# A decoder trunk on one core: the split parts of the feed-forward weights start at 256 pairs of places instead of one

## The chip, the core and the metric

The kernel runs on one core of one Trainium2 chip. The metric is the device time of one execution in microseconds. TensorE (PE in the profile) multiplies; its weight loads are counted apart as PEld; ScalarE is ACT, VectorE is DVE, GpSimd is POOL, SyncE (SP) issues the transfers.

## The reference

Four layers of a decoder on 256 tokens of 1024 features, all float32. Each layer adds half a SwiGLU feed-forward, a mixer (stick-breaking attention, MoBA, multi-head latent attention, then stick-breaking again) and a second half feed-forward; a norm closes the trunk.

```python
def swiglu(x, w_gate_up, w_down):
    g, u = jnp.split(x @ w_gate_up, 2, axis=-1)
    return (jax.nn.silu(g) * u) @ w_down
...
    for i in range(DEPTH):
        h = h + 0.5 * swiglu(rms_norm(h, norm_ffn1[i]), ffn1_w_gate_up[i], ffn1_w_down[i])
        hn = rms_norm(h, norm_mix[i])
...
        h = h + mix
        h = h + 0.5 * swiglu(rms_norm(h, norm_ffn2[i]), ffn2_w_gate_up[i], ffn2_w_down[i])
    return rms_norm(h, final_norm)
```

D_FF is 2816, so a layer's two feed-forwards hold most of the products.

## The kernel before

**Float32 by two parts.** TensorE multiplies in float32r. Every weight w is split exactly into a high part (ScalarE copies it into a float32r buffer, line 314) and a low part (VectorE subtracts the high part from w, line 321). The activations are split the same way. A product is hi·hi + hi·lo + lo·hi.

**Chunks and pieces.** Weights come in chunks of up to 128 x 2048 values, one transfer each, into one of four `raw` buffers (line 225). `Chunk` (lines 284 to 333) cuts a chunk into two pieces; each takes one of six pairs `whi`/`wlo` of 1024 columns (`parts`, line 226). Every piece starts at column 0 of both its buffers, and row block k stands at k·w from there (`get`, lines 324 to 327).

**The feed-forward's products** (`wide`, lines 432 to 435). For each pair of a 128 x 128 block of weights and a 128-row block of activations there are two matmuls, each with a weight load of its own: the high part against high and low activations side by side (512 columns, line 434), then the low part against the high activations (256 columns, line 435). `x2` holds the normed input so (8 row blocks), `a2` the gated activations (22 row blocks). Gate-up walks 22 chunks of 8 row blocks x 2 column blocks, down 16 chunks of 11 row blocks, in each of 8 feed-forwards: 8 x (352 + 176) = 4224 pairs of matmuls.

```python
def wide(o, wh, wl, m2, first, last):
    nc.tensor.matmul(o, wh, m2.rearrange("p a b -> p (a b)"), start=first, stop=False, skip_group_check=True)
    nc.tensor.matmul(o[:, :SEQ], wl, m2[:, 0, :], start=False, stop=last, skip_group_check=True)
```

**The mixers' products.** `w_proj` with `mm3` (lines 426 to 430) has weights stationary and three matmuls of 256 columns to a block. `x_proj` (lines 462 to 480; its matmuls are lines 475 to 477) has the activations stationary and the split weights moving, 288 to 512 columns wide.

**Places in SBUF.** Tiles are laid out in the order in which they are made, each start rounded up to 32 bytes: `raw`, `parts`, `mids`, `probs`, `nats` (5), `turned`, `squares` (2), `gh`, and then `x2` and `a2`. All before `gh` are whole multiples of 256 bytes long; `gh` takes 8628 bytes, rounded to 8640, which is 192 more than a multiple of 256. So, counted modulo 256 bytes, a weight block stands 64 bytes after the row block of `x2` or `a2` that it is multiplied with, for the high and the low part alike, in all of the feed-forward and in `w_proj`; in `x_proj`, where the roles are exchanged, the stationary operand stands 192 bytes after the moving one.

**Order.** `Program.emit` lists the instructions by estimated costs, at build time: each engine's next is the ready one with the lowest priority number. Buffers taken and given back (`Slots`) are part of it, so a room with fewer buffers can change the order. `square` (line 340) takes one of the `squares` for each row block of a norm's sum of squares; line 345 adds it up, and lines 403 to 408 make the norm from it. `nats` serves the attention's operands and the result.

Of the kernel before, what the change touches and what calls it, by code (L numbers as in the profile page):

```python
# [28 lines left out]
ZC = SEQ + P  # columns of a head's scores that causality leaves  # L29
# [10 lines left out]
HALF = MAXC // 2  # L40

# Gains in one table, 128 rows of a norm to a column.
# [9 lines left out]
class Slots:  # L52
    """Room for a number of like buffers; some of them are kept from work that can wait."""

    def __init__(self, aps):
        self.aps = list(aps)
        self.free = list(range(len(self.aps)))
# [11 lines left out]
class Buf:  # L69
    """A buffer that the first op of its use takes and the last one gives back."""  # L70
# [7 lines left out]
class Op:  # L78
    """A run of instructions: `ways` has its cost and its emitter for each engine that can do it."""
# [6 lines left out]
class Program:  # L86
    """The program as a graph of short runs of instructions. `emit` puts them in order by a list
    scheduling on estimated costs: each engine's next is the ready one with the least priority
    number, which is the tensor engine's nominal time (us) at the op's place."""
# [32 lines left out]
    def copy(self, cols, fn, deps=(), n=1, **kw):  # L122
        """fn(engine's copy) by whichever of ScalarE and VectorE comes to it first."""
        return self.either({"ACT": (n * 0.095 + 0.00083 * cols, lambda: fn(self.on_act)),
                            "DVE": (n * 0.07 + 0.00104 * cols, lambda: fn(self.on_dve))}, deps, **kw)

    def emit(self):
# [3 lines left out]
        events = []  # time, number, op that becomes ready or buffer that becomes free  # L131
# [58 lines left out]
def fast(n, cols=SEQ):  # L190
    """Time of n float32r products."""
    return n * (max(cols, 256) / 2400 + 0.0025)
# [3 lines left out]
def trunk_kernel(ctx: ExitStack, tc: tile.TileContext, a: dict, out: bass.AP, nsub: int = 3 * DEPTH):  # L196
# [23 lines left out]
    # ---- room on the chip  # L220
    def room(n, shape, name, dt=F32):
# [4 lines left out]
    parts = Slots([(cp.tile([P, HALF], F32R, name=f"whi{i}"), cp.tile([P, HALF], F32R, name=f"wlo{i}"))  # L226
                   for i in range(6)])
    mids = room(3, [2 * ZC], "mid")
    probs = room(2, [2, ZC], "prob")
    nats = room(5, [512], "nat")  # L230
    turned = room(4, [4, SEQ], "turned")
    squares = room(2, [SEQ], "sq")
# [3 lines left out]
    # The normed rows and the activations: a row block's high parts, then its low ones.  # L236
    x2 = cp.tile([P, NT, 2, SEQ], F32R, name="x2")
    a2 = cp.tile([P, NF, 2, SEQ], F32R, name="a2")
# [6 lines left out]
    # In a mixer the activations' room holds the heads' outputs, then split softplus or latents.  # L245
# [11 lines left out]
    # ---- the tensor engine's clock rises with work: zeros, until the first data come  # L257
# [6 lines left out]
    # ---- constants  # L264
# [8 lines left out]
    # jp[p, i] = i - p  # L273
# [9 lines left out]
    # ---- the weights: DMA, then an exact split of each float32 value into two float32r parts  # L283
    class Chunk:
        """`n` row blocks of `w` columns, `per` of them to a piece. The program's first chunks come
        and are split in smaller runs of row blocks, between `cuts`, the loads in the order `lead`."""

        def __init__(self, ap, n, w, per, cuts=None, lead=20.0):
            self.w, self.per = w, per
            self.pieces = []  # L290
            self.ready = [None] * n
            raw = Buf(raws)
            load = None if cuts else self.load(ap, raw, 0, n, lead)
            for i in range(0, n, per):
                b = Buf(parts)
                self.pieces.append(b)
                end = min(n, i + per)
                ks = [k for k in cuts or () if i <= k < end] or [i]
                for k, e in zip(ks, ks[1:] + [end]):
                    o = load or self.load(ap, raw, k, e, lead - 3.0 * k)  # L300
                    hi = g.act((e - k) * w, self.hi_fn(raw, b, i, k, e), [o], take=[b] if k == i else [])
                    lo = g.dve((e - k) * w, self.lo_fn(raw, b, i, k, e), [hi], free=[raw])
                    for j in range(k, e):
                        self.ready[j] = lo
# [7 lines left out]
        def hi_fn(self, raw, b, i, k, e):  # L312
            w = self.w
            return lambda: nc.scalar.activation(b.ap[0][:, (k - i) * w:(e - i) * w], raw.ap[:, k * w:e * w], AF.Copy)  # L314

        def lo_fn(self, raw, b, i, k, e):
            w = self.w

            def f():
                s = slice((k - i) * w, (e - i) * w)  # L320
                nc.vector.tensor_sub(b.ap[1][:, s], raw.ap[:, k * w:e * w], b.ap[0][:, s].bitcast(F32))  # L321
            return f

        def get(self, k):
            s = slice(k % self.per * self.w, (k % self.per + 1) * self.w)
            hi, lo = self.pieces[k // self.per].ap
            return hi[:, s], lo[:, s]
# [10 lines left out]
    # ---- norms  # L338
    def square(m, dep, lead):
        """Row block m's share of the mean square; gives the op that adds it."""  # L340
        if m == 0:
            return g.act(SEQ, lambda: nc.scalar.activation(acc, h[:, m, :], AF.Square), [dep], lead=lead)
        b = Buf(squares)
        s = g.act(SEQ, lambda: nc.scalar.activation(b.ap, h[:, m, :], AF.Square), [dep], take=[b], lead=lead)
        return g.dve(SEQ, lambda: nc.vector.tensor_add(acc, acc, b.ap), [s, state["acc"]], free=[b], lead=lead)  # L345

    def prep(m, gain_at, dep, start=False):
        """Row block m of h is final: its gained, split form for the next products, or its share
        of the result, still to be divided by the rms."""
# [12 lines left out]
    def result(m, dep):  # L362
        """Row block m, gained, transposed into the banks of the result."""
# [14 lines left out]
    def rsqrt(v, scale, keep):  # L378
        """(v * scale + EPS) ** -0.5 of a [128, 2] tile, by Newton's method."""
# [3 lines left out]
        # x is -1/2 of the radicand; the first guess comes from its bits.  # L383
# [11 lines left out]
    def norm(scales):  # L395
        """1 / rms of the tokens: as columns (`r`) and along the rows, times the scales (`rb`).
        Gives the ops that make them."""
# [23 lines left out]
    def table(name):  # L421
        """Loads ScalarE's functions, after the last use of those before."""
        state["table"] = g.op("ACT", 1.3, lambda: nc.scalar.preload_act_table_set(name), state["last"], lead=4.0)
        state["last"] = []

    def mm3(o, wh, wl, mh, ml, first, last):
        """o += wh.T @ mh + wh.T @ ml + wl.T @ mh"""
# [4 lines left out]
    def wide(o, wh, wl, m2, first, last):  # L432
        """The same, with the products of the moving operand's low parts in the bank's other half."""
# [6 lines left out]
    def both(o, b, last, take=(), lead=0.0):  # L440
        """o() = the sum of the bank's halves."""
# [3 lines left out]
    def w_proj(chunk, xs, xdeps, keep=0, step=2):  # L445
        """Products with two column blocks of a chunk stationary: a bank [128, 2 x 256], and the
        last op."""
# [14 lines left out]
    def x_proj(chunks, n, cols, xs, xdeps, keep=0):  # L462
        """Products with the activations stationary: two banks [128 tokens, cols], and the last op."""
# [18 lines left out]
    # ---- feed-forward  # L482
    def ffn(l, which, g_next):
# [5 lines left out]
        def gate_up(j, cuts, lead, step):  # L489
            c = Chunk(gu[l, j], NT, 2 * P, NT // 2, cuts, lead)  # L490
# [36 lines left out]
        for m in range(NT):  # L527
            b = bank()
            last = None
            for half in range(2):  # L530
                c = Chunk(dn[l, m, half], FH, P, 6)
# [16 lines left out]
    # ---- shared by the mixers  # L548
    def out_proj(w_o, ot, g_next):
        """The heads' outputs times w_o, onto h."""  # L550
# [9 lines left out]
    def mask_in(o, mask):  # L560
        """The mask of the two diagonal blocks, 256 columns apart."""
# [3 lines left out]
    def head_out(t, p, pdeps, vdeps):  # L565
        """The weighted values of pair t; p: transposed weights [128, 2, 384], keys 0-127 of the 256
        queries, then keys 128-255 of queries 128-255."""
# [18 lines left out]
    # ---- stick-breaking attention  # L586
    def sb_pair(t, s, sdep, vdeps):
        """s: queries and keys of a pair of heads, transposed."""
# [91 lines left out]
    def v_out(half, bs, last, r, n):  # L680
        """Values in their natural layout, times 1 / rms."""
# [3 lines left out]
    # ---- softmax attention of a pair of heads  # L685
    def softmax_pair(t, q, k, deps, vdeps, scale, used):
        """q, k: for each of the two heads, [d, 256] transposed queries and keys."""
# [61 lines left out]
    def rotate(x, cs, n):  # L749
        """Rotary embedding in place: x [128, heads, n], cs: [128, 2, n] (cos twice, sin twice)."""  # L750
# [12 lines left out]
    def turn_heads(x, deps, n, rows, d):  # L763
        """Four blocks of `rows` columns of x[t], transposed, into the tile d."""
# [14 lines left out]
    # ---- MoBA attention: one block holds the sequence, so no past block is ever valid  # L779
# [38 lines left out]
    # ---- multi-head latent attention  # L818
    def mix_mla(j, g_next):
# [3 lines left out]
        # The latents' gained, split, transposed forms.  # L823
# [100 lines left out]
    # ---- the trunk  # L924
# [19 lines left out]
    # ---- the last norm  # L944
# [19 lines left out]
def layouts(x, norm_ffn1, ffn1_w_gate_up, ffn1_w_down, norm_mix, norm_ffn2, ffn2_w_gate_up, ffn2_w_down, sb_w_qkv,  # L964
            sb_w_o, moba_w_qkv, moba_w_o, mla_w_in, mla_q_norm, mla_w_uq, mla_kv_norm, mla_w_ukv, mla_w_o, final_norm):
    """The inputs as the program reads them: every load is of long rows."""
# [14 lines left out]
    for n, gu, dn in (("ffn1", ffn1_w_gate_up, ffn1_w_down), ("ffn2", ffn2_w_gate_up, ffn2_w_down)):  # L981
        # layer, row block, row, gate or up, column block, column
# [8 lines left out]
    def halves(w):  # L991
        """Row blocks in two runs of four, columns in two halves: half, run, row, block, column."""
        return w.reshape(w.shape[0], 2, 4, P, 2, 512).transpose(0, 4, 1, 3, 2, 5).reshape(w.shape[0], 2, 2, P, 2048)

    def outs(w):
        """Pairs of column blocks: pair, row, row block, column of the pair."""
# [44 lines left out]
```

## Time and profile before

| what | value |
|---|---|
| median of 2 runs | 1964.29 us (1962.36 to 1966.22) |
| profiled execution, first to last instruction | 1960.8 us |
| PE busy | 1946.6 us (99%) |
| PEld busy | 1696.5 us (87%) |
| DVE busy | 1452.3 us (74%) |
| ACT busy | 1144.1 us (58%) |

The two runs and the profiled execution are different executions: the runs lie 1.6 to 5.4 us above the profiled span. Matmul records are modelled at their end and reach past the start of the next one, so a matmul's own cost is the distance from its start to the next start.

### The profile page before, as it was taken

The numbers are of one execution on the slowest core, as the hardware profiler recorded it, in microseconds if no ns is written. First come the engines' busy times: TensorE is split into PE (matmuls) and PEld (weight loads), VectorE is DVE, ScalarE is ACT, GpSimd is POOL, SyncE is SP. The second block draws the span as 40 slices with busy tenths as digits, with TensorE's granted clock in tenths as the row PEclk, the third lists the DMA queues.
The fourth block names the chain that finished last, engine by engine and source line by source line (L and its number), as shares of the span: only waits on it lengthen the run. The fifth ranks groups of instructions, "written<-read, shape, count | busy, mean of one in ns | idle before, by whom it ended". The sixth has DMA issues, their size and how long they took to land.

```text
span 1960.8 us, 30578 instructions
## 1 busy us (share of the span) xinstructions
PE 1946.6 (99%) x11681; PEld 1696.5 (87%) x11681; DVE 1452.3 (74%) x2661; ACT 1144.1 (58%) x2119; POOL 0.4 (0%) x5
## 2 busy tenths in 40 slices
PE   9999999999999999999999999999999999999997
PEld 7888989888888878888888888988888888898886
DVE  8777767777777777877677768877677766668864
ACT  7555556555555555655555557755555555665553
POOL 0000000000000000000000000000000000000000
PEclk9999999999999999999999999999999999999999
DMA  8546435546654653554655454355465456435542
GB/s 301 184 146 220 163 129 175 191 147 204 208 181 147 221 181 109 178 188 147 214 199 191 141 178 155 126 197 178 151 213 197 165 168 220 148 125 198 177 151 81
DMA packets 55875, 342.79 MB, mean 175 GB/s; under 512 B 6192, under 2 KB 7088, under 8 KB 26928
## 3 DMA queue, kind: packets, MB, share of 16 engines
q1 hardware_dynamic: 55728, 340.84, 50.6%
q8 instruction: 92, 1.51, 0.3%
q14 instruction: 55, 0.45, 0.1%
HBM read 339.76 MB, written 1.05 MB: 174 GB/s over the span
## 4 chain that ended last, share of the span: by engine, by line
PE 98%; ACT 1%; DVE 0%; DMA 0%; SPq 0%; issue 0%; DVEq 0%; ACTq 0%
PE ps L434 50%; PE ps L435 26%; PE ps L428 3%; PE ps L429 3%; PE ps L430 3%; PE ps L475 3%; PE ps L476 2%; PE ps L477 2%; PE ps L574 1%; PE ps L624 1%; PE ps L733 1%; PE ps L698 1%; PE ps L771 1%; PE ps L596 1%; PE ps L562 0%; PE ps L576 0%
## 5 line engine op out<-in xcount | busy, mean ns | idle before, releaser
L314 ACT ACTIVATE whi<-raw 128x1024 fp32r<-128x1024 f32 (+2 forms) x738 | 703.0, 954 | 729.7 <-PE ps L434 527.3
L321 DVE TENSOR_TENSOR wlo<-raw,whi 128x1024 fp32r<-128x1024 f32 (+2 forms) x738 | 804.2, 1091 | 396.7 <-ACT whi L314 388.6
L434 PE MATMUL ps<-x,whi 128*128 128x512 f32 x2816 | 998.3, 398 | 1.0 <-DVE acc L345 0.8
L435 PE MATMUL ps<-x,wlo 128*128 128x256 f32 x2816 | 791.8, 281 | 0.2 <-DVE wlo L321 0.2
L434 PEld LDWEIGHTS ps<-x,whi 128*128 128x128 f32 x2816 | 529.7, 188 | 132.2 <-ACT whi L314 2.5
L435 PEld LDWEIGHTS ps<-x,wlo 128*128 128x128 f32 x2816 | 528.8, 188 | 1.3 <-DVE wlo L321 1.2
L434 PE MATMUL ps<-a,whi 128*128 128x512 f32 x1408 | 498.8, 398 | 0.0
L435 PE MATMUL ps<-a,wlo 128*128 128x256 f32 x1408 | 395.7, 281 | 0.0
L434 PEld LDWEIGHTS ps<-a,whi 128*128 128x128 f32 x1408 | 264.8, 188 | 65.1
L435 PEld LDWEIGHTS ps<-a,wlo 128*128 128x128 f32 x1408 | 264.4, 188 | 0.0
L443 DVE TENSOR_TENSOR mid<-ps,mid 128x256 f32<-128x256 f32 x416 | 173.5, 417 | 9.6 <-ACT mid L442 9.6
L442 ACT ACTIVATE mid<-ps 128x256 f32<-128x256 f32 x416 | 151.3, 367 | 11.9 <-PE ps L435 11.9
L515 DVE TENSOR_TENSOR mid<-mid 128x256 f32<-128x256 f32 x176 | 74.6, 424 | 14.2 <-DVE mid L443 0.5
L510 DVE TENSOR_TENSOR mid<-mid,rb 128x256 f32<-128x256 f32 x176 | 74.7, 424 | 6.4 <-ACT rb L411 0.9
L475 PE MATMUL ps<-whi,x 128*128 128x512 f32 (+2 forms) x192 | 74.4, 388 | 0.0
L517 DVE TENSOR_TENSOR a<-mid,a 128x256 fp32r<-128x256 f32 x176 | 73.4, 418 | 1.0 <-ACT a L516 1.0
L428 PE MATMUL ps<-a,whi 128*128 128x256 f32 x256 | 73.9, 289 | 0.0
L428 PE MATMUL ps<-x,whi 128*128 128x256 f32 x256 | 73.0, 285 | 0.0
L476 PE MATMUL ps<-wlo,x 128*128 128x512 f32 (+2 forms) x192 | 72.9, 380 | 0.0
L511 ACT ACTIVATE mid<-mid 128x256 f32<-128x256 f32 x176 | 71.8, 408 | 1.8 <-DVE mid L510 1.7
L477 PE MATMUL ps<-whi,x 128*128 128x512 f32 (+2 forms) x192 | 72.7, 379 | 0.0
L429 PE MATMUL ps<-a,whi 128*128 128x256 f32 x256 | 71.5, 279 | 0.0
(128 smaller groups left out, 1636.7 us busy)
## 6 DMA issues: line engine op xcount, KB each, us to landing
raw<-in_ffn_gu SPq DMA_DIRECT2D x173, 1024.0 KB, 4.8
raw<-in_ffn_dn SPq DMA_DIRECT2D x128, 704.0 KB, 4.1
raw<-in_sb_qk SPq DMA_DIRECT2D x16, 1024.0 KB, 4.9
raw<-in_moba_qkv SPq DMA_DIRECT2D x12, 1024.0 KB, 4.8
raw<-in_sb_v SPq DMA_DIRECT2D x8, 1024.0 KB, 4.7
raw<-in_sb_o SPq DMA_DIRECT2D x8, 1024.0 KB, 4.7
raw<-in_moba_o SPq DMA_DIRECT2D x4, 1024.0 KB, 4.8
raw<-in_mla_o SPq DMA_DIRECT2D x4, 1024.0 KB, 5.0
```

What stands on the lines that cost most here:

```text
L314: return lambda: nc.scalar.activation(b.ap[0][:, (k - i) * w:(e - i) * w], raw.ap[:, k * w:e * w], AF.Copy)
L321: nc.vector.tensor_sub(b.ap[1][:, s], raw.ap[:, k * w:e * w], b.ap[0][:, s].bitcast(F32))
L428: nc.tensor.matmul(o, wh, mh, start=first, stop=False, skip_group_check=True)
L429: nc.tensor.matmul(o, wh, ml, start=False, stop=False, skip_group_check=True)
L434: nc.tensor.matmul(o, wh, m2.rearrange("p a b -> p (a b)"), start=first, stop=False, skip_group_check=True)
L435: nc.tensor.matmul(o[:, :SEQ], wl, m2[:, 0, :], start=False, stop=last, skip_group_check=True)
L442: x = g.act(SEQ, lambda: nc.scalar.activation(o(), b.ap[:, SEQ:], AF.Copy), [last], take=take, lead=lead)
L443: return g.dve(SEQ, lambda: nc.vector.tensor_add(o(), b.ap[:, :SEQ], o()), [x], free=[b], lead=lead)
L475: nc.tensor.matmul(o, xs[0][:, k, ts], hi, start=(k == 0), stop=False)
L476: nc.tensor.matmul(o, xs[0][:, k, ts], lo, start=False, stop=False)
L477: nc.tensor.matmul(o, xs[1][:, k, ts], hi, start=False, stop=(k == n - 1))
L510: o = g.dve(SEQ, lambda: nc.vector.tensor_mul(x(), x(), rb[:, 0, :]), [o, rbs[0]])
```

## The change

Each `whi` and `wlo` buffer becomes 64 columns (256 bytes) longer, and a piece starts at a place in it: one of 16 starts, 4 columns (16 bytes) apart, for the high part and one for the low part. `place(i)` gives the i-th of the 256 pairs. Gate-up's pieces go through them in order, the high part's place changing from piece to piece (2 x 176 = 352 pieces, so 96 pairs come twice); down's 256 pieces go through them with the two parts exchanged. All mixers' pieces have the pair (48, 0): the high part 192 bytes in, the low part at the start. `x2` and `a2` move up, right behind `parts`; as the longer buffers are still multiples of 256 bytes, a place is now the distance, modulo 256 bytes, from the row block of activations to the block of weights. To make room, `nats` goes from 5 buffers to 4 and `squares` from 2 to 1.

```diff
+PAD = 64
...
-    parts = Slots([(cp.tile([P, HALF], F32R, name=f"whi{i}"), cp.tile([P, HALF], F32R, name=f"wlo{i}"))
+    parts = Slots([(cp.tile([P, HALF + PAD], F32R, name=f"whi{i}"), cp.tile([P, HALF + PAD], F32R, name=f"wlo{i}"))
                    for i in range(6)])
+
+    x2 = cp.tile([P, NT, 2, SEQ], F32R, name="x2")
+    a2 = cp.tile([P, NF, 2, SEQ], F32R, name="a2")
...
-    nats = room(5, [512], "nat")
+    nats = room(4, [512], "nat")
...
-    squares = room(2, [SEQ], "sq")
+    squares = room(1, [SEQ], "sq")
...
-    x2 = cp.tile([P, NT, 2, SEQ], F32R, name="x2")
-    a2 = cp.tile([P, NF, 2, SEQ], F32R, name="a2")
...
+            self.places = places or [(48, 0)] * (n // per + 1)
...
-            return lambda: nc.scalar.activation(b.ap[0][:, (k - i) * w:(e - i) * w], raw.ap[:, k * w:e * w], AF.Copy)
+            w, o = self.w, self.places[i // self.per][0]
+            return lambda: nc.scalar.activation(b.ap[0][:, o + (k - i) * w:o + (e - i) * w], raw.ap[:, k * w:e * w], AF.Copy)
...
-                nc.vector.tensor_sub(b.ap[1][:, s], raw.ap[:, k * w:e * w], b.ap[0][:, s].bitcast(F32))
+                oh, ol = self.places[i // self.per]
+                n = (k - i) * w, (e - i) * w
+                nc.vector.tensor_sub(b.ap[1][:, ol + n[0]:ol + n[1]], raw.ap[:, k * w:e * w],
+                                     b.ap[0][:, oh + n[0]:oh + n[1]].bitcast(F32))
...
             hi, lo = self.pieces[k // self.per].ap
-            return hi[:, s], lo[:, s]
+            at = k % self.per * self.w
+            oh, ol = self.places[k // self.per]
+            return hi[:, oh + at:oh + at + self.w], lo[:, ol + at:ol + at + self.w]
...
+    def place(i):
+
+        return 4 * (i % 16), 4 * (i // 16)
...
-            c = Chunk(gu[l, j], NT, 2 * P, NT // 2, cuts, lead)
+            at = 2 * ((2 * l + which) * NF + j)
+            c = Chunk(gu[l, j], NT, 2 * P, NT // 2, cuts, lead, [place(at % 256), place((at + 1) % 256)])
...
-                c = Chunk(dn[l, m, half], FH, P, 6)
+                at = 2 * (((2 * l + which) * NT + m) * 2 + half)
+                c = Chunk(dn[l, m, half], FH, P, 6, None, 20.0, [place(at)[::-1], place(at + 1)[::-1]])
```

The number of instructions is the same on every engine, and so are the shapes. On PE the order changes only within the first feed-forward's first five chunks. Before, the first norm's sum (the two matmuls of `onesf` and `acc`) stood after the fourth chunk:

```order
L434 MATMUL ps_68<-x_107,whi_84 128x512
L435 MATMUL ps_68<-x_107,wlo_85 128x256
L434 MATMUL ps_69<-x_107,whi_84 128x512
L435 MATMUL ps_69<-x_107,wlo_85 128x256
L403 MATMUL ps_70<-onesf,acc 128x1 x2
L434 MATMUL ps_71<-x_107,whi_86 128x512
L435 MATMUL ps_71<-x_107,wlo_87 128x256
```

Now it stands twelve matmuls later, among those of the chunk that follows (lines 439, 440 and 408 are the former 434, 435 and 403):

```order
L439 MATMUL ps_71<-x_90,whi_86 128x512
L440 MATMUL ps_71<-x_90,wlo_87 128x256
L408 MATMUL ps_72<-onesf,acc 128x1 x2
L439 MATMUL ps_70<-x_90,whi_86 128x512
L440 MATMUL ps_70<-x_90,wlo_87 128x256
L439 MATMUL ps_71<-x_90,whi_86 128x512
L440 MATMUL ps_71<-x_90,wlo_87 128x256
```

No other matmul changes its place among the weights' products. On ACT, at the same time of the program, squares and splits before:

```order
L354 ACTIVATE x_107<-gh 128x256 x2
L344 ACTIVATE sq_105<-gh 128x256
L314 ACTIVATE whi_78<-raw_74 128x512
L344 ACTIVATE sq_104<-gh 128x256
L314 ACTIVATE whi_80<-raw_75 128x512
L354 ACTIVATE x_107<-gh 128x256 x2
```

With a single square buffer two splits follow each other (lines 359, 349 and 316 are the former 354, 344 and 314):

```order
L359 ACTIVATE x_90<-gh 128x256 x2
L349 ACTIVATE sq_105<-gh 128x256
L316 ACTIVATE whi_78<-raw_74 128x512
L316 ACTIVATE whi_80<-raw_75 128x512
L349 ACTIVATE sq_105<-gh 128x256
L359 ACTIVATE x_90<-gh 128x256 x2
```

The square that stood between the two splits comes after them.

## Rows read from the trace of the kernel before

**Rows 1.** The page, part 1: busy time by engine, share of the span.
```profile
span 1960.8 us, 30578 instructions
PE 1946.6 (99%) x11681; PEld 1696.5 (87%) x11681; DVE 1452.3 (74%) x2661; ACT 1144.1 (58%) x2119; POOL 0.4 (0%) x5
```

**Rows 2.** The page, part 4: the chain that ended last, by engine and line.
```profile
PE 98%; ACT 1%; DVE 0%; DMA 0%; SPq 0%; issue 0%; DVEq 0%; ACTq 0%
PE ps L434 50%; PE ps L435 26%; PE ps L428 3%; PE ps L429 3%; PE ps L430 3%; PE ps L475 3%; PE ps L476 2%; PE ps L477 2%; PE ps L574 1%; PE ps L624 1%; PE ps L733 1%; PE ps L698 1%; PE ps L771 1%; PE ps L596 1%; PE ps L562 0%; PE ps L576 0%
```

**Rows 3.** Waits of PE: total us, times, longest us.
```profile
PE ps L434 <- DVE acc L345: 0.8, 1, 0.8
...
PE ps L435 <- DVE wlo L321: 0.2, 1, 0.2
```

**Rows 4.** Line 434 in 440 to 490 us: ns min/median/max, first and last start.
```profile
L434 PE MATMUL ps<-a,whi x143: 397/397/398, 439.7 to 489.9; 128*128 128x512 f32 x143
```

**Rows 5.** Timeline of a feed-forward from 501 us: start us, us, instruction.
```profile
501.06 0.28 PE L435 MATMUL ps<-x,wlo 128*128 128x256 f32 x1
501.06 0.19 PEld L434 LDWEIGHTS ps<-x,whi 128*128 128x128 f32 x1
501.17 0.40 PE L434 MATMUL ps<-x,whi 128*128 128x512 f32 x1
501.18 0.19 PEld L435 LDWEIGHTS ps<-x,wlo 128*128 128x128 f32 x1
501.41 0.28 PE L435 MATMUL ps<-x,wlo 128*128 128x256 f32 x1
```

**Rows 6.** Groups by line and form: xcount | busy us, mean ns | idle before.
```profile
L434 PE MATMUL ps<-x,whi 128*128 128x512 f32 x2816 | 998.3, 398 | 1.0 <-DVE acc L345 0.8
L435 PE MATMUL ps<-x,wlo 128*128 128x256 f32 x2816 | 791.8, 281 | 0.2 <-DVE wlo L321 0.2
L321 DVE TENSOR_TENSOR wlo<-raw,whi 128x1024 fp32r<-128x1024 f32 x456 | 557.5, 1224 | 229.9 <-ACT whi L314 228.0
L434 PE MATMUL ps<-a,whi 128*128 128x512 f32 x1408 | 498.8, 398 | 0.0
L435 PE MATMUL ps<-a,wlo 128*128 128x256 f32 x1408 | 395.7, 281 | 0.0
L443 DVE TENSOR_TENSOR mid<-ps,mid 128x256 f32<-128x256 f32 x416 | 173.5, 417 | 9.6 <-ACT mid L442 9.6
L517 DVE TENSOR_TENSOR a<-mid,a 128x256 fp32r<-128x256 f32 x176 | 73.4, 418 | 1.0 <-ACT a L516 1.0
```

**Rows 7.** PE groups in 271 to 275.2 us (`w_proj`).
```profile
L428 PE MATMUL ps<-x,whi 128*128 128x256 f32 x13 | 3.6, 276 | 0.0
```

**Rows 8.** PE groups in 297.5 to 307 us (`w_proj`).
```profile
L428 PE MATMUL ps<-a,whi 128*128 128x256 f32 x28 | 7.9, 281 | 0.0
```

**Rows 9.** PE groups in 1701.3 to 1708.1 us (`x_proj`).
```profile
L476 PE MATMUL ps<-wlo,x 128*128 128x512 f32 x11 | 4.3, 394 | 0.0
L475 PE MATMUL ps<-whi,x 128*128 128x512 f32 x11 | 4.3, 392 | 0.0
L477 PE MATMUL ps<-whi,x 128*128 128x512 f32 x10 | 3.9, 388 | 0.0
```

**Rows 10.** Busy time in 30 to 130 us (gate-up).
```profile
core 0: us, PE busy (x) PEld busy (x) DVE busy (x) ACT busy (x) POOL busy (x), PEclk, DMA share, GB/s
30.00:130.00 100.00, 100.00 (x568) 86.83 (x567) 77.57 (x129) 57.91 (x109) 0.00 (x0) 1.00 0.54 188
```

**Rows 11.** Groups by line and form in the mixers, whole span.
```profile
L429 PE MATMUL ps<-a,whi 128*128 128x256 f32 x256 | 71.5, 279 | 0.0
...
L476 PE MATMUL ps<-wlo,x 128*128 128x512 f32 x160 | 62.8, 392 | 0.0
```

More of the change, by code (lines that the diff above doesn't have):

```diff
@@ L284, in trunk_kernel, with __init__ @@
     class Chunk:
-        def __init__(self, ap, n, w, per, cuts=None, lead=20.0):
+        def __init__(self, ap, n, w, per, cuts=None, lead=20.0, places=None):
             self.w, self.per = w, per
+            self.places = places or [(48, 0)] * (n // per + 1)
             self.pieces = []
@@ L312, in hi_fn @@
         def hi_fn(self, raw, b, i, k, e):
-            w = self.w
-            return lambda: nc.scalar.activation(b.ap[0][:, (k - i) * w:(e - i) * w], raw.ap[:, k * w:e * w], AF.Copy)
+            w, o = self.w, self.places[i // self.per][0]
+            return lambda: nc.scalar.activation(b.ap[0][:, o + (k - i) * w:o + (e - i) * w], raw.ap[:, k * w:e * w], AF.Copy)
         def lo_fn(self, raw, b, i, k, e):
@@ L319, in f @@
             def f():
-                s = slice((k - i) * w, (e - i) * w)
-                nc.vector.tensor_sub(b.ap[1][:, s], raw.ap[:, k * w:e * w], b.ap[0][:, s].bitcast(F32))
+                oh, ol = self.places[i // self.per]
+                n = (k - i) * w, (e - i) * w
+                nc.vector.tensor_sub(b.ap[1][:, ol + n[0]:ol + n[1]], raw.ap[:, k * w:e * w],
+                                     b.ap[0][:, oh + n[0]:oh + n[1]].bitcast(F32))
             return f
         def get(self, k):
-            s = slice(k % self.per * self.w, (k % self.per + 1) * self.w)
             hi, lo = self.pieces[k // self.per].ap
-            return hi[:, s], lo[:, s]
+            at = k % self.per * self.w
+            oh, ol = self.places[k // self.per]
+            return hi[:, oh + at:oh + at + self.w], lo[:, ol + at:ol + at + self.w]
         def used(self, ks):
```

## The prediction

> **What bounds the kernel now.** I read the busy shares first, then the chain, then PE's waits. PE is busy for 1946.6 of 1960.8 us [rows 1], and the chain that ended last is PE for 98%, of which lines 434 and 435, the feed-forward's products, are 76% [rows 2]. PE hardly waits for anyone: its longest waits on splits or norms are 0.8 and 0.2 us, once each, at the start [rows 3]. So an edit counts only if it changes how fast matmuls follow each other, or slows VectorE or ScalarE until PE starts to wait.
>
> How fast they follow is the second reading. In a feed-forward 143 matmuls of line 434 start between 439.7 and 489.9 us: 50.2/142 = 353.5 ns for a pair (512 and 256 columns) [rows 4]. The timeline shows how it divides: 0.24 us from the 512-wide start to the next start, 0.11 to 0.12 from the 256-wide one, and each weight load runs while the matmul before it runs [rows 5]. The record of a 512-wide matmul is 398 ns long and of a 256-wide one 281 [rows 6], some 163 ns beyond the next start in both cases. I take that tail as fixed, so a record that is 5 ns shorter means a pitch that is 5 ns shorter.
>
> Now the same shapes elsewhere. The 256-wide matmul of `w_proj` has records of 276 ns in one stretch [rows 7] and of 281 in another [rows 8]. The 512-wide one of `x_proj` has 388, 392 and 394 [rows 9], mean 391.3. The granted clock is 1.00 (the upper level, 2.4 GHz) in the gate-up stretch that I looked at [rows 10]. So the feed-forward's matmuls stand at the slow end of what these shapes do in this trace, by up to 10 ns for 512 columns and 5 for 256. The place of operands is one thing that could make the difference: the feed-forward has its weights 64 bytes after the moving rows (modulo 256), `x_proj` has 192. It is not the only one: `w_proj` has both 276 and 281 at one and the same distance of 64.
>
> **The change part by part.**
>
> *Feed-forward pieces at 256 pairs of places.* 4224 pairs of matmuls, 8448 weight loads (2816 + 1408 of each line, [rows 6]). Nothing in the trace has these pairs of places. Lower end: both matmuls as short as the shortest rows, 388 and 276, so (398 - 388) + (281 - 276) = 15 ns a pair, 4224 x 15 = 63 us gained. Middle: the means of the other shapes, 391.3 and 278.5, give 6.7 + 2.5 = 9.2 ns, 39 us gained. No effect of places: 0. On the other side no steady row is above 398 and 281, so the trace gives no price for a bad place; I bound it by a load that is no longer hidden at one of the 16 distances, 8448/16 = 528 loads, each for the pitch of the shortest matmul that carries a whole load, 276 - 163 = 113 ns, so 60 us lost. Between -63 and +60 I take half of the middle, 4224 x 4.6 = 19 us gained. Reason: an average over all places should lie inside what the shapes do and not at the slow end, where the one pair in use lies now; but `w_proj` shows that part of that difference is not the place.
>
> A rule of the Trainium skill speaks against any gain. The page "TensorE: Matmul & The Clock Gate", Part 2, "Step-by-step: what each phase is for", says that PE has two independent SBUF read ports, one for the moving operand and one for the weight load, so that loading the next weights takes nothing from the running matmul. By that rule no place costs or gives anything and this term is 0; the trace agrees that loads run beside matmuls [rows 5], and leaves open why one shape has records from 388 to 398 ns.
>
> *Mixer pieces at (48, 0).* `w_proj` then has distances 192 and 0 instead of 64, `x_proj` 64 and 0 instead of 192. 1536 matmuls of `w_proj` average about 279 [rows 11]: all at 276 would give 1536 x 3 = 4.6 us, all at 281 would cost 3.1. Of `x_proj` 480 are 512 wide, at 392 [rows 11]: at 388 they give 1.9 us, at 398 they cost 2.9. Together -7 to +6; I take 0.
>
> *The splits at shifted starts.* ScalarE and VectorE do the same instructions. A split of 1024 columns takes VectorE 1224 ns [rows 6]. In 100 us of gate-up VectorE is busy for 77.57 [rows 10]; a chunk lasts 16 pairs x 353.5 ns = 5.66 us and has two splits, so 35 splits share 22.4 idle us: each may grow by 0.64 us, to 1.86, before VectorE binds. A shift of 64 bytes between operands shows nothing: line 517 works on `a2` and `mids`, which are off by that much, in 418 ns, line 443 on aligned tiles and PSUM in 417 [rows 6]. I take 0, hidden under PE.
>
> *One square buffer, four `nats`.* Squares then alternate with VectorE's sums. In the trunk the norm's row is needed only after the next products have begun, and PE's order does not change there. At the start two splits follow each other at once, where a square stood between: PE's waits of 0.8 and 0.2 us [rows 3] are what this can give, and a square more in front of the norm is what it can cost. I take -0.5, bounds -1 to +2.
>
> **The sum.** -19 + 0 + 0 - 0.5 = about -20 us, on a profiled span of 1960.8: 1941. The median of the runs lies 3.5 us above that span, so 1964.3 - 20 = 1944 us.
>
> **The rivals.**
>
> *No effect of places.* For it: `w_proj` has two pitches at one distance, and the rule above says so. Against it: one shape has records from 388 to 398 ns in one program, at two different distances. Time: 1964.
>
> *The places free the feed-forward wholly.* If most pairs of places are as good as the other shapes' rows, the gain is 39 to 63 us: 1901 to 1925, more than 2% (39.3 us, about what a measurement of this kernel can tell from no change). For it: the feed-forward sits at the slow end for its whole length, 398 and 281 as means over thousands of records [rows 6], like a fixed pattern that any shift would break. Against it: 256-wide matmuls fall into the 281 pattern at times whatever came before.
>
> *A bad distance.* The other side: at some distances the weight load and the moving rows meet in the same part of SBUF, and the load is not hidden any more. Place: the feed-forward's loads. Price: 113 ns a load. It decides from 39.3/0.113 = 348 loads on, 4% of 8448, so a single bad distance of the 16 is enough: 1964 + 60 = 2024 us. For it: only two of the 16 distances are in the trace, and distance 0, where both start in the same place, is not. Against it: neither of these two, nor any steady row, shows a load that stands in the open.
>
> VectorE as the new bound would need splits half as long again; I count it with the bad distance.
>
> **How the numbers follow.** Forecast (a gain by about half of the middle, 1925 to 1964) 0.40; no effect 0.26; wholly free 0.21; bad distance 0.13. The first two lie within 2%: 0.66. Faster is 0.21, slower 0.13. The range goes from 1902 (the lower end of the sum) to 1988, beyond no effect and the small costs; it leaves out most of the bad distance. The likeliest case alone: 1925 to 1964. Predicted 1944.
>
> **What would show it.** Right: PE still 99% busy with the same chain; records of lines 439 and 440 (the former 434 and 435) no longer all 398 and 281 but varying from piece to piece, in stretches of 8 to 16 pairs, with a mean between 388 and 398 and between 276 and 281; gate-up stages shorter by some 1%. No effect: the same two numbers in all pieces. Bad distance: a share of 1 in 16 with much longer records and weight loads. Wrong altogether: VectorE above 95% in gate-up and PE waiting for `wlo`, or records above 398 in most pieces.

## The result and the profile after

The changed kernel runs in 1951.78 us (median of 2 runs, 1951.72 to 1951.84) against 1964.29 before: ratio 0.9937, 95% interval 0.9919 to 0.9956. That is 0.6% faster: clear of no change by its interval, and within the 2% called the same. Predicted were 1944 us, with a range of 1902 to 1988. Executions of one kernel differ by up to 4 us, and in six of the thirteen traces of this document, not in the two compared here, the granted clock is 0.50 (the lower level, 1.2 GHz) instead of 1.00 for 3.4 us that begin 11 to 13 us after the start.

The profiled execution spans 1950.1 us, 10.7 less than before. The page's busy times and its chain, the counterpart of [rows 1, 2]:

```profile
span 1950.1 us, 30511 instructions
PE 1935.1 (99%) x11681; PEld 1694.9 (87%) x11681; DVE 1450.4 (74%) x2661; ACT 1146.0 (59%) x2119; POOL 0.4 (0%) x5
...
PE 98%; ACT 1%; DVE 0%; DMA 0%; SPq 0%; issue 0%; DVEq 0%; ACTq 0%
```

PE bounds the kernel as before, and nearly the whole difference lies in how fast matmuls follow each other. The groups by line and form (busy us, mean ns of one, idle before) are the counterpart of [rows 6, 11]; 439 and 440 are the former 434 and 435, 433 to 435 the former 428 to 430, 480 to 482 the former 475 to 477:

```profile
L439 PE MATMUL ps<-x,whi 128*128 128x512 f32 x2816 | 987.2, 395 | 1.7 <-DVE acc L350 1.4 <-ACT whi L316 0.3
L440 PE MATMUL ps<-x,wlo 128*128 128x256 f32 x2816 | 788.4, 280 | 0.2 <-DVE wlo L324 0.2
L324 DVE TENSOR_TENSOR wlo<-raw,whi 128x1024 fp32r<-128x1024 f32 x456 | 557.3, 1223 | 223.8 <-ACT whi L316 222.1
L439 PE MATMUL ps<-a,whi 128*128 128x512 f32 x1408 | 493.3, 394 | 0.0
L440 PE MATMUL ps<-a,wlo 128*128 128x256 f32 x1408 | 394.1, 280 | 0.0
L435 PE MATMUL ps<-a,wlo 128*128 128x256 f32 x256 | 72.4, 283 | 0.0
L434 PE MATMUL ps<-a,whi 128*128 128x256 f32 x256 | 71.8, 281 | 0.0
L481 PE MATMUL ps<-wlo,x 128*128 128x512 f32 x160 | 63.6, 397 | 0.0
```

In the feed-forward the records fell from 398 to 395 and 394, and from 281 to 280. In the mixers they rose: line 434 (the former 429) from 279 to 281, line 481 from 392 to 397. The split of 1024 columns takes as long as before (1223 ns against 1224).

The same stretch of a feed-forward as in [rows 4] (ns min/median/max, first and last start) and the gate-up stretch of [rows 10]:

```profile
L439 PE MATMUL ps<-a,whi x144: 388/394/403, 439.7 to 489.7; 128*128 128x512 f32 x144
```
```profile
30.00:130.00 100.00, 100.00 (x575) 87.57 (x574) 79.95 (x134) 60.49 (x113) 0.00 (x0) 1.00 0.54 192
```

Where every record was 397 or 398, they now go from 388 to 403, and a pair takes 50.0/143 = 349.7 ns instead of 353.5. The clock is 1.00 in both, and VectorE at 80% is far from binding.

Taken apart by the first and last matmul of each stage, the 16 feed-forward stages (8 gate-up, 8 down) are 15.9 us shorter (gate-up from 1004.4 to 993.9, down from 500.3 to 494.9), the four mixers between them 4.9 us longer (from 441.9 to 446.8), and the end 0.3 us longer: -15.9 + 4.9 + 0.3 = -10.7.

A piece lasts 8 pairs in gate-up, so the two windows below each lie inside one piece: first the pair of places (16, 4) at its second visit, then (16, 16), the distance of before (groups of PE in the window, busy us, mean ns).

```profile
L439 PE MATMUL ps<-x,whi 128*128 128x512 f32 x6 | 2.1, 389 | 0.0
L440 PE MATMUL ps<-x,wlo 128*128 128x256 f32 x5 | 1.4, 276 | 0.0
```
```profile
L439 PE MATMUL ps<-x,whi 128*128 128x512 f32 x6 | 2.2, 396 | 0.0
L440 PE MATMUL ps<-x,wlo 128*128 128x256 f32 x6 | 1.7, 281 | 0.0
```

The first is within 1 ns of the shortest rows of before, 388 and 276; the second is close to the old 398 and 281. From start to start the means of the pairs of places go from 340.5 ns a pair of matmuls to 355.2; the mean over all 256 is 349.4.

### The profile page after: what moved, and what is told of

Read it like the earlier page. It is cut to its first block, busy times and chain, and to the rows that moved or that the text cites. A ratio compares the mean times of both kernels' runs of the same rounds, so it can differ in the third digit from the quotient of the medians.

```text
span 1950.1 us, 30511 instructions
## 1 busy us (share of the span) xinstructions
PE 1935.1 (99%) x11681; PEld 1694.9 (87%) x11681; DVE 1450.4 (74%) x2661; ACT 1146.0 (59%) x2119; POOL 0.4 (0%) x5
## 4 chain that ended last, share of the span: by engine, by line
PE 98%; ACT 1%; DVE 0%; DMA 0%; SPq 0%; issue 0%; DVEq 0%; ACTq 0%
PE ps L439 50%; PE ps L440 25%; PE ps L433 3%; PE ps L435 3%; PE ps L434 3%; PE ps L480 3%; PE ps L481 2%; PE ps L482 2%; PE ps L585 1%; PE ps L635 1%; PE ps L744 1%; PE ps L709 1%; PE ps L782 1%; PE ps L607 1%; PE ps L573 0%; PE ps L587 0%
## 5 line engine op out<-in xcount | busy, mean ns | idle before, releaser
L439 PE MATMUL ps<-x,whi 128*128 128x512 f32 x2816 | 987.2, 395 | 1.7 <-DVE acc L350 1.4
L439 PE MATMUL ps<-a,whi 128*128 128x512 f32 x1408 | 493.3, 394 | 0.0
L440 PE MATMUL ps<-a,wlo 128*128 128x256 f32 x1408 | 394.1, 280 | 0.0
L433 PE MATMUL ps<-a,whi 128*128 128x256 f32 x256 | 73.7, 288 | 0.0
L435 PE MATMUL ps<-a,wlo 128*128 128x256 f32 x256 | 72.4, 283 | 0.0
```

The lines of the kernel that those rows point to most:

```text
L433: nc.tensor.matmul(o, wh, mh, start=first, stop=False, skip_group_check=True)
L435: nc.tensor.matmul(o, wl, mh, start=False, stop=last, skip_group_check=True)
```

## Experiments

Three theories stood at first. D: the distance from the moving rows to the weights, modulo 256 bytes, sets the pitch. P: it is the change of place from piece to piece that breaks a slow pattern. L: the gain came from the layout, the order or the rooms. All edits below are to the changed kernel, unless said otherwise.

**One fixed pair for the whole feed-forward, four times.** The edit, here for the first; the others have (16, 16), (16, 4) and (24, 44) in its place, and the second and third also have (16, 16) as the mixers' pair:

```diff
-        return 4 * (i % 16), 4 * (i // 16)
+        return 48, 0
...
-                c = Chunk(dn[l, m, half], FH, P, 6, None, 20.0, [place(at)[::-1], place(at + 1)[::-1]])
+                c = Chunk(dn[l, m, half], FH, P, 6, None, 20.0, [place(at), place(at + 1)])
```

> All feed-forward pieces at the one pair (48, 0), as the mixers' pieces already are: high part 192 bytes after the activations modulo 256, low part 0. Theory D (the distance of each part from the moving rows sets the pitch): in the changed kernel the pieces at this pair ran at 340.6 ns a pair of matmuls against 353.4 before, so 4224 x 12.8 = 54 us less than before, and 5 us more in the mixers: about 1915 us, records near 389 and 276. Theory P (it is the change of place from piece to piece that breaks a slow pattern): one fixed pair falls back to 353.4, about 1969 us. Theory L (the gain came from the new layout, order or rooms, not from the places): as the changed kernel, 1952 us.

> All pieces, the mixers' too, at (16, 16): the layout, the order and the rooms of the changed kernel, but every distance is again 64 bytes as in the kernel before. Theory D: the pitch of before, 353.4 ns a pair, records 398 and 281, and the mixers as before: 1964 us within 3. Theory P: the same. Theory L: 1952 us or less, since the layout is kept.

> All feed-forward pieces at (16, 4), high part 64 bytes and low part 16 bytes on, the mixers' pieces at (16, 16) as before. Theory D: the pieces at this pair ran at 340.5 ns a pair in the changed kernel, so 4224 x 12.9 = 54 us less than before and the mixers as before: about 1910 us. Theory P: 1964 us. Theory L: 1952 us.

> All feed-forward pieces at (24, 44), the pair with the longest pitch in the changed kernel (355.2 ns), the mixers at (48, 0). Theory D: 4224 x 1.8 = 8 us more than before and 5 us more in the mixers: about 1977 us. Theory P: about 1969 us. Theory L: 1952 us.

| feed-forward, mixers | us | ratio to before, interval |
|---|---|---|
| (48, 0), (48, 0) | 1939.2 | 0.9875, 0.986 to 0.989 |
| (16, 16), (16, 16) | 1964.8 | 1.0001, 0.9991 to 1.001 |
| (16, 4), (16, 16) | 1909.6 | 0.9724, 0.971 to 0.9739 |
| (24, 44), (48, 0) | 1943.4 | 0.9896, 0.9881 to 0.991 |

The 512-wide matmuls of the same 50 us of a down stage, for (16, 16), then for (16, 4), whose stage ends at 485 us:

```profile
L439 PE MATMUL ps<-a,whi x143: 397/397/398, 439.7 to 489.8; 128*128 128x512 f32 x143
```
```profile
L439 PE MATMUL ps<-a,whi x134: 389/389/389, 439.8 to 485.0; 128*128 128x512 f32 x134
```

(16, 16) has the layout, the order and the rooms of the changed kernel and the distances of the old one, and its records are those of [rows 4], to the nanosecond. L falls. (16, 4) differs from it by 48 bytes in the place of the feed-forward's low parts and by nothing else, and gains 55 us: a pair of matmuls takes 45.2/133 = 339.8 ns (340.0 over a whole down stage, against 353.3 at (16, 16)), record after record the same 389. A fixed place does that, so P falls as well. It is faster than the kernel before and the changed one.

D holds for these two to 1 us, and misses the other two: (48, 0) should have come to 1915 and came to 1939, (24, 44) to 1977 and came to 1943. So the sweep's number for a single pair of places need not be what that pair does when it stays.

**The rooms and the order alone.** The kernel before with `nats` at 4 and `squares` at 1:

```diff
-    nats = room(5, [512], "nat")
+    nats = room(4, [512], "nat")
...
-    squares = room(2, [SEQ], "sq")
+    squares = room(1, [SEQ], "sq")
```

> The kernel before with only the rooms changed: 4 nats instead of 5, 1 square instead of 2; no places, x2 and a2 at the end of the layout as before (1024 + 2048 bytes earlier, so still 64 bytes off). It has the order of the changed kernel. Theory D (distances alone): as before, 1964 us, within 2. Theory L (order or rooms have a share in the gain): below 1962 us, by as much as that share.

1964.1 us, ratio 1.0002 (0.9993 to 1.0011): no share in the gain that this can show.

**The mixers' places alone.** The sweep stays, the mixers' pieces go back to the old distance:

```diff
-            self.places = places or [(48, 0)] * (n // per + 1)
+            self.places = places or [(16, 16)] * (n // per + 1)
```

> The changed kernel with its sweep in the feed-forward, but the mixers' pieces at (16, 16), the distance of before. Theory D: the mixers' stages took 4.9 us longer in the changed kernel than before (1.5 + 1.8 + 0.3 + 1.3); these come back, so 1952 - 5 = 1947 us. If the mixers' loss came from what the sweep leaves behind (state, order), nothing comes back: 1952 us.

1948.1 us, ratio 0.9921 (0.9908 to 0.9935), 3.6 us less than the changed kernel's 1951.8. Line 434 in its groups:

```profile
L434 PE MATMUL ps<-a,whi 128*128 128x256 f32 x256 | 71.7, 280 | 0.0
L434 PE MATMUL ps<-x,whi 128*128 128x256 f32 x256 | 71.3, 278 | 0.0
```

They are back at 278 to 280, and the four stretches between the stages take 442.5 us, against 446.8 in the changed kernel and 441.9 before: 4.3 of the 4.9 us come back. The mixers' loss is that of their pair (48, 0).

**Distance or address.** Both kernels put 64 bytes ahead of `x2`. The first moves all places by 64 bytes too, so that distances stay as with (16, 4) and addresses do not; the second leaves the feed-forward's weights at (16, 4), so that their addresses stay and the distances do not.

```diff
+    cp.tile([P, 16], F32, name="shift")
     x2 = cp.tile([P, NT, 2, SEQ], F32R, name="x2")
```

> As the run with (16, 4) and mixers (16, 16), but x2 and a2 start 64 bytes later, and so do all places: (32, 20) and (32, 32). All distances between weights and activations are those of that run, all addresses are other ones modulo 256. Distance theory: the same time, 1910 us, 340 ns a pair. Address theory (each operand's own address modulo 256 counts): some other pitch between 340 and 355 ns, 1910 to 1973 us, most likely near the mean of the sweep, 349, so 1947 us.

> As the run with (16, 4), the weights at the same addresses, but x2 and a2 start 64 bytes later (mixers at (32, 32), which keeps their distance at 64). The distances in the feed-forward become 0 and 208 bytes instead of 64 and 16, while high and low part keep theirs from each other. Distance theory: the pitch of the pair (0, 52), 348.9 ns in the sweep, so 1964 - 4224 x 4.5 = 1945 us, within the 350 and 340 that a fixed pair may lock to. If only the weights' addresses or the distance of the high from the low part count: 340 ns, 1910 us.

1909.0 us (ratio 0.9725, 0.971 to 0.974) and 1945.5 us (0.9909, 0.9895 to 0.9922). The matmuls of the first and the second in the same window (line 440 is 439 here):

```profile
L440 PE MATMUL ps<-a,whi x133: 389/389/389, 439.8 to 484.7; 128*128 128x512 f32 x133
```
```profile
L440 PE MATMUL ps<-a,whi x145: 392/393/396, 439.6 to 489.9; 128*128 128x512 f32 x145
```

Same distances, other addresses: the same 389. Same weight addresses, same distance between high and low part, other distance to the moving rows: 392 to 396. So it is the distance between the weights and the rows that stream past them that counts, in this test by a shift of 64 bytes. The second run is also where the sweep was right about a pair that stays: 348.9 ns both times.

**The same pair in all shapes.** Mixers at (16, 4) as well:

> All pieces, the mixers' too, at (16, 4). The feed-forward as with mixers at (16, 16): 340 ns a pair, 1909.6 us in all. If the pair is good for every shape, w_proj goes from a mean pitch of 116 to 113.3 ns and x_proj from 229 to 227: 1536 x 2.6 + 696 x 2 = 5 us less, about 1904 us. If a distance is good for one order of matmuls only, the mixers move by up to 5 us either way: 1905 to 1915 us.

1912.6 us (0.9735, 0.9719 to 0.9751), about 3 us more than with the mixers at (16, 16), though the two intervals overlap. The traces are clearer: the stretches between the stages take 444.8 us instead of 442.3, and in `w_proj` the records are longer than the 278 that the mixers at (16, 16) have just shown:

```profile
L434 PE MATMUL ps<-x,whi 128*128 128x256 f32 x256 | 72.0, 281 | 0.0
```

A pair that is good for 512 and 256 columns in turn is not good for three times 256.

**Why (48, 0) and (24, 44) miss.** In the trace of (48, 0) the feed-forward has two pitches, each for nearly whole stages. The first line is from the third gate-up stage, the second from the sixth (the last count of such a line is that of a sample):

```profile
L439 PE MATMUL ps<-x,whi x273: 395/395/396, 514.7 to 609.9; 128*128 128x512 f32 x137
...
L439 PE MATMUL ps<-x,whi x280: 389/389/390, 1284.9 to 1379.7; 128*128 128x512 f32 x140
```

Start to start this is 350.0 ns in the first five feed-forwards and 340.0 in the last three, but for stretches of up to 32 pairs of matmuls at the start of some gate-up stages, at one and the same pair of places. Two more runs went after that. In the first only the mixers' pair is another one, (16, 16); in the second the first two chunks of each feed-forward stand at (16, 4) as well:

```diff
-            c = Chunk(gu[l, j], NT, 2 * P, NT // 2, cuts, lead, [place(at % 256), place((at + 1) % 256)])
+            c = Chunk(gu[l, j], NT, 2 * P, NT // 2, cuts, lead, [(16, 4)] * 2 if j < 2 else [place(at % 256), place((at + 1) % 256)])
```

> Feed-forward at (48, 0), mixers at (16, 16). With the mixers at (48, 0) the feed-forward ran at 350.0 ns a pair until the third mixer and at 340.0 after it, for whole stages. If the distance alone set the pitch, one value would hold throughout; if the pitch is a pattern that is caught when a stage begins and then kept, the stages divide otherwise between 340 and 350 now that other work stands before them, and the time lies between 1964 - 54 = 1910 us (all at 340) and 1964 - 14 = 1950 us (all at 350).

> As the run with (48, 0) in the feed-forward and (16, 16) in the mixers, but the first two chunks of every feed-forward stand at (16, 4), the pair that ran at 340 ns everywhere. If the pitch of (48, 0) is a pattern that is caught and then kept, all stages start from the fast one and stay in it: 340 ns from the first feed-forward on, about 1910 us instead of 1934. If the change from 350 to 340 ns at the third mixer has another cause (what runs, or what data stand, from there on), the first five stages still run at 350: about 1934 us.

The first gave 1933.9 us (0.9847, 0.9832 to 0.9862), with the same division as in the run at (48, 0) everywhere: the places of the mixers' weights did not change it, against what the pattern theory expected. The second gave 1933.1 us (0.9839, 0.9823 to 0.9855), neither the 1910 of a pattern that always stays fast nor the old division. After two slow feed-forwards, fast and slow ones now alternate. Its third gate-up stage, slow in both runs before, and its sixth, fast in both:

```profile
L439 PE MATMUL ps<-x,whi x295: 389/389/389, 509.7 to 609.7; 128*128 128x512 f32 x148
...
L439 PE MATMUL ps<-x,whi x292: 395/395/395, 1274.6 to 1376.5; 128*128 128x512 f32 x146
```

So the third mixer alone is not the cause. The same pieces with the same data take either pitch, though nothing was changed but the places of the first two chunks of each feed-forward. The timeline of its second gate-up stage (start us, us) shows a pattern being left, inside these first chunks at (16, 4), where the norm's small matmuls stand between:

```profile
317.07 0.39 PE L439 MATMUL ps<-x,whi 128*128 128x512 f32 x1
317.30 0.28 PE L440 MATMUL ps<-x,wlo 128*128 128x256 f32 x1
317.42 0.39 PE L439 MATMUL ps<-x,whi 128*128 128x512 f32 x1
317.65 0.28 PE L440 MATMUL ps<-x,wlo 128*128 128x256 f32 x1
317.76 0.50 PE L408 MATMUL ps<-onesf,acc 128*128 128x1 f32 x4
318.12 0.48 PE L439 MATMUL ps<-x,whi 128*128 128x512 f32 x1
...
318.56 0.39 PE L439 MATMUL ps<-x,whi 128*128 128x512 f32 x1
318.78 0.28 PE L440 MATMUL ps<-x,wlo 128*128 128x256 f32 x1
318.90 0.39 PE L439 MATMUL ps<-x,whi 128*128 128x512 f32 x1
```

Ahead of it the steps are 0.35 us a pair (346.7 ns over the nine pairs before 317.42), behind it 0.34 (340.1 over the ten from 318.56 on). So (16, 4) did not run at 340 ns everywhere, as the last expectation has it. In its own run, too, it begins each gate-up stage behind a mixer at 347 ns. The pair (24, 44) begins these stages at 360.0 ns and goes over to 346.7 behind the norm's last small matmuls. Here are (16, 4), (48, 0) and (24, 44) at the start of the second gate-up stage of their first runs, then (24, 44) and (48, 0) further on in it:

```profile
L439 PE MATMUL ps<-x,whi x16: 392/392/392, 305.7 to 310.9; 128*128 128x512 f32 x16
L439 PE MATMUL ps<-x,whi x17: 389/389/389, 311.3 to 316.7; 128*128 128x512 f32 x17
L439 PE MATMUL ps<-x,whi x16: 402/402/403, 310.9 to 316.3; 128*128 128x512 f32 x16
...
L439 PE MATMUL ps<-x,whi x316: 393/393/393, 322.7 to 431.9; 128*128 128x512 f32 x158
L439 PE MATMUL ps<-x,whi x316: 395/395/396, 322.6 to 432.9; 128*128 128x512 f32 x158
```

This explains (24, 44) as well: the sweep met it twice, for five and for eight pairs of matmuls, once near either pitch (347.5 and 358.4 ns), and the mean of these few made it the longest; when it stays, the short pitch holds for all but the starts of the first gate-up stage and of those behind mixers.

The traces also show where the pitch changes. Each gate-up stage has two breaks, the norm's sums (line 408) and its two transposes (line 413). Behind a mixer they stand after the 20th and the 32nd pair of matmuls, behind another feed-forward after the 20th and the 28th, in the first feed-forward after the 38th and the 52nd. With (48, 0) throughout, the pitch changes within a few pairs of one of these breaks and nowhere else in the seven gate-up stages after the first, and the pitch behind the transposes goes on through the down stage.

In the last run (16, 4) holds for the first 32 pairs. Where a feed-forward follows another one, the transposes leave four pairs of it; these run at 340 ns, and (48, 0) takes 340 over and keeps it, all three times. Where it follows a mixer, (48, 0) begins right behind the transposes, at 350 ns, all four times, and in the first feed-forward the transposes stand well inside (48, 0), with 350 on both sides. So the fast pattern was kept wherever it ran when the places changed, and the miss of 23 us comes from the other five. That is read from the traces; no run moves the norm's matmuls. Why the transposes leave 350 ns behind them in five feed-forwards of the runs at (48, 0) and 340 in the last three stays open.

## Why the prediction was right, and where it was not

*What bounds the kernel.* Right: PE at 99%, the same chain, and no new wait but one of 0.3 us at the start.

*The sum.* Forecast were about 20 us; the medians give 12.5 and the traces 10.7. Between the traces, 3.6 of the missing 8.8 us are the feed-forward with its start (-19.5 forecast, -15.9 measured), 4.9 the mixers and 0.3 the end.

*The feed-forward's places.* Forecast 4.6 ns a pair and 19 us; measured 15.9/4224 = 3.8 ns and 15.9 us. The reason given, that an average over all places lies inside what the shapes do and the pair in use lies at the slow end, is what the pieces show: 349.4 on average, between 340.5 and 355.2, with the old distance at 353.3 when it stays. The tail taken as fixed bears out: from (16, 16) to (16, 4) the two records lose 8 and 5 ns and the pitch 13.3. The half taken off was argued from `w_proj`'s two pitches at one distance; the runs at (48, 0) show two pitches at one distance in the feed-forward too. That it should be a half, no row said: that 19 lies so near 15.9 is luck in part.

*No effect of places.* Refuted by (16, 16) against (16, 4): 48 bytes, 55 us. The rule of the Trainium skill weighed there (page "TensorE: Matmul & The Clock Gate", Part 2, "Step-by-step: what each phase is for") says that loading the next weights takes nothing from the running matmul. What the prediction drew from it, that no place costs or gives anything, does not hold for these products; the measurement decides. Whether the rule itself fails is not shown: that reads of weights and of moving rows get in each other's way is my reading of the distance that matters, and no run separates the load from the rest.

*The mixers.* This is the term that was mis-sized: 0 was taken between bounds of -7 and +6, and it was +4.9, of which 4.3 us came back when their pair was undone. I had taken gains and losses to cancel with no row for it; `w_proj` and the 512-wide matmuls of `x_proj` both lost.

*Splits, rooms, order.* The splits are right at 0: 1223 ns for 1024 columns. The gain of 0.5 us from the order did not come: PE's waits on splits and the norm, 0.8 and 0.2 us before, are 1.4, 0.3 and 0.2 after, and with the rooms alone the kernel took 1964.1 us.

*The places free the feed-forward wholly.* Not with the sweep, but with one pair that stays: (16, 4) gains 55 us, inside the 39 to 63 worked out for it. The rows of other products gave that floor rightly, 389 and 276 against 388 and 276. The argument against it, that the 281 pattern comes at times whatever came before, had no row; in the feed-forward what stands before does bear on the pitch, as the runs at (48, 0) show.

*A bad distance.* Did not come: in the sweep no pair of places has a mean above 355.2 ns, and the longest pitch that was kept, 360.0 ns at (24, 44) behind a mixer, is 6.7 ns above (16, 16); a load in the open had been priced at 113.

## To carry to other kernels

Where PE is full and the same shape has different record lengths in different stretches, the place of the stationary operand against the moving one is worth a few runs, even 16 bytes of it; shift one of them alone and keep everything else. Judge a place by a kernel that keeps it throughout: pieces of 8 pairs of matmuls showed the average rightly, but of the five pairs of places tried they missed (48, 0) by 9 ns in five feed-forwards of eight, and (24, 44) by 8.5. Look also behind other matmuls that break the stream, for that is where the pitch changes. Tune each shape for itself, as the pair that is best for one order of matmuls lengthens the records of another.

## What was not expected of the hardware

The pitch of a pair of matmuls stands at steps that it keeps for hundreds of pairs: over whole down stages 340.0 ns at (16, 4), 346.7 at (24, 44), 353.3 at (16, 16), and 350.0 and 340.0 at (48, 0). At the granted 1.00, the upper level of 2.4 GHz, these are 816, 832, 848 and 840 clocks, all of them multiples of 8. As far as these runs go, the distance decides which pitches can come; (16, 16) comes back to its one behind every break, and at the other three pairs of places two were seen. And it repeats: the piece at (16, 4) in the first feed-forward and the one 1420 us later have the same records, 389 and 276. The first of the two, in the changed kernel from 64.9 us:

```profile
L439 PE MATMUL ps<-x,whi 128*128 128x512 f32 x7 | 2.4, 389 | 0.0
L440 PE MATMUL ps<-x,wlo 128*128 128x256 f32 x6 | 1.7, 276 | 0.0
```
